# Two matmuls and a fold in place of three matmuls for 28 of layer 0's projections

## Chip, cores and metric

The kernel runs on one core of one Trainium2 chip. The metric is the device time of one execution in microseconds (us); the time before is the median of three runs.

## The reference

A two-layer decoder trunk over 256 tokens of width 2048, all in float32. Layer 0 is what the change touches:

```python
def recurrent_mixers(h, w_in, ...):
    proj = h @ w_in                                   # 2048 -> 6144 columns
    x_lru, y_lru, q_h, f_h, v_h, g_h = jnp.split(proj, list(IN_SPLITS), axis=-1)
    lru = rg_lru(causal_depthwise_conv(x_lru, conv_w, conv_b), w_a, b_a, w_i, b_i, lam)
    lru = lru * jax.nn.gelu(y_lru.astype(F32), approximate=True)
    hg = hgrn2(q_h, f_h, v_h, g_h, lower_bound, g_norm)   # 8 heads of 128 columns
    return jnp.concatenate([lru, hg], axis=-1) @ w_out
```

`h` is the RMS-normed input. `hgrn2` is a gated linear recurrence with a 128x128 state per head. A residual add and a squared-ReLU MLP follow; layer 1 has attention in the mixer's place.

## The kernel before

Every float32 product is made of float32r parts: a weight unit (one tile of 128x2048, 1 MB) is loaded to `raw`, ACT casts it to `hi` (L117) and DVE forms `lo = raw - hi` (L118), each in two halves in layer 0. The activations stand in `bufa` as `[hi | lo]`, 256 columns each. A product keeps hi*hi, hi*lo and lo*hi. `raw`, `hi` and `lo` have three buffers each, so the cast of one unit waits until PE has read the `hi` of the unit three before it, and the subtraction waits for that unit's `lo`.

A projection of layer 0 (`project`, for one block of 128 output features) takes one unit: 16 weight blocks of 128x128, each the stationary operand against 256 token columns. Two helpers do it. `direct` runs three matmuls of 256 columns per block, all into columns 0 to 255 of a PSUM bank `p`. `cross` runs one matmul of 512 columns for the block's `hi` (both halves of the activation at once, over the whole bank) for all 16 blocks, and then one of 256 columns for each block's `lo`, into the bank's second half; the two halves of the bank must be added afterwards. That fold is in `scaled`: ACT copies the second half to `t1` (L443), DVE adds the first (L444) and multiplies by the norm's factor (L445). After `direct` one DVE multiplication (L440) is all. Before, all of layer 0 uses `direct`; layer 1's q and k projections use `cross`.

The steps of layer 0 stand in the string `ORDER`: `v0 h0 x0 h1 x1 h2 x2 h3 x3 v1 h4 x4 h5 x5 h6 x6 h7 x7 g0 y0 y1 y2 y3 g1 y4 y5 y6 y7`. `h` is a head of `hgrn` (three projections: q, f, g), `x` an input block of the RG-LRU (one projection, `lru_in`), `y` its gate branch, `g` the two groups of recurrence gates, `v` the values of four heads each, computed by token (two banks at once, 96 matmuls of 512 columns). The projections, gates and value groups are chained in this order on PE (`mm`). A head's own small matmuls are not: L475, seven levels of L491, L486, L515 to L517 and the transposes L529 are put among the projections by a scheduler, which writes one fixed order for every engine. Between two levels of a head DVE updates the head's mask result (L494) and its operand `qk` (L508); the levels 32 and 64 are copied into `st` by ACT (L499, L501), the last by L487.

The banks: pool `pmm` has three, used in turn by projections, gates and value groups; pool `psc` has two named `pl` for the levels (also used by half of the gates of `g1`) and one each of `po`, `pd` and `pt`. The values of `v0` and `v1` share one buffer `vg`, so ACT's read-out of `v1`'s two banks (L361) waits until head 3's last products with the old values (L516, L517) are through.

Of the kernel before, what the change touches and what calls it, by code (L numbers as in the profile page):

```python
# [41 lines left out]
def trunk_kernel(ctx, tc, head, x, xtok, cols, tab, masks, pos, fin, w_in, w_gate, w_out, w_qkv, w_o, w1, w2, out):  # L42
# [154 lines left out]
    def unit(src, i):  # L197
        u = at[1]
        assert units[u][0] is src and units[u][1] in (None, i), (u, i)
        at[1] += 1  # L200
        if u + 2 >= at[0]:
            fetch()
        return made.pop(u)
# [54 lines left out]
            mm(p, h, mov[:, S:], start=False, stop=False)  # L258
            mm(p, l, mov[:, :S], start=False, stop=last)

    HA, XA, YA = direct, direct, direct

    def split_to(dst, src, gain=None):
        if gain is None:
            h, l = dst[..., :S], dst[..., S:]
            A.copy(h, src)
            V.tensor_tensor(l, src, h.bitcast(F32), OP.subtract)  # L267
        else:
            A.activation(dst[:, :S], src, AF.Copy, scale=gain)  # L269
            V.scalar_tensor_tensor(dst[:, S:], src, gain, dst[:, :S].bitcast(F32),  # L270
                                   op0=OP.mult, op1=OP.subtract)
# [92 lines left out]
    def project(src, i, mov, acc=None):  # L364
        w = unit(src, i)
        p = pmm.tile([P, 512], F32, name="p")
        jobs = [(k, mov[:, k], k == 0, k == KB - 1) for k in range(KB)]
        (acc or cross)(p, w, jobs)
        return p
# [67 lines left out]
    def scaled(p, z, acc=None):  # L437
        with urgent():
            if acc is direct:
                V.tensor_tensor(z, p[:, :S], rs, OP.mult)  # L440
            else:
                t = wk.tile([P, S], F32, name="t1", bufs=2)
                A.copy(t, p[:, S:])  # L443
                V.tensor_tensor(z, p[:, :S], t, OP.add)  # L444
                V.tensor_tensor(z, z, rs, OP.mult)  # L445
# [10 lines left out]

    def hgrn(hd, vg):
        u0 = 18 + (hd // 4) * 16 + (hd % 4) * 3
        oml = omlb[:, hd:hd + 1]
        qk = wk.tile([P, 2 * S], F32, name="qk", bufs=3)  # L460
        qp, kq = qk[:, :S], qk[:, S:]
# [76 lines left out]
    xc = wk.tile([P, 8, S], F32, name="xc", bufs=1)  # L538

    def lru_in(b):  # L540
        p = project(w_in, b, bufa, XA)
        xp = wk.tile([P, S + 4], F32, name="xp", bufs=1)
        V.memset(xp[:, :4], 0.0)
        scaled(p, xp[:, 4:], XA)
        A.activation(xc[:, b], xp[:, 4:], AF.Identity, bias=col("conv_b", b), scale=col("conv_w", 24 + b))
        for i in range(3):
            V.scalar_tensor_tensor(xc[:, b], xp[:, 1 + i:1 + i + S], col("conv_w", 8 * i + b), xc[:, b],
                                   op0=OP.mult, op1=OP.add)
        split_to(bufb[:, b], xc[:, b])
# [39 lines left out]
    for step in ORDER.split():  # L589
        i = int(step[1])  # L590
        if step[0] == "v":
            vgroups[i] = tokens_group(w_in, 30, rt) if i else vfirst
        elif step[0] == "h":
            hgrn(i, vgroups[i // 4])
        else:
            {"x": lru_in, "y": lru_out, "g": lru_gates}[step[0]](i)
# [557 lines left out]
```

## Time and profile before

| | |
|---|---|
| median of 3 runs | 2142.7 us (2142.47 to 2142.79) |
| profiled execution | 2142.28 us, span 2140.5 us |
| busy PE / PE weight loads / DVE / ACT | 2129.8 / 1826.2 / 1823.9 / 1280.6 us |
| granted TensorE clock | 0.999 |
| HBM read | 485.95 MB, 228 GB/s over the span |

PE starts layer 0's projections at 28.3 us and ends them at about 331 us. How to read the rows: "busy" of PE counts pipelined matmuls whose ends are modelled, so what a matmul costs is read from the distance between starts. An arrow `<-` behind an idle time names what ended it. In the timeline, equal instructions that follow each other are one row with `xN`.

### The profile page before, as it was taken

How to read it: one execution, taken by the hardware profiler on the slowest of the kernel's cores; microseconds unless marked ns; L12 is line 12 of the kernel's file. 1: busy time of each engine (PE TensorE's matmuls, PEld its weight loads, DVE VectorE, ACT ScalarE, POOL GpSimd, SP SyncE). 2: the span in 40 equal slices, each digit the busy share in tenths (PEclk: the TensorE clock that was granted, in tenths of full speed). 3: DMA queues.
4: the chain of work that ended last, by engine and by line, in shares of the span. 5: the costliest groups of instructions: out<-in, count | busy, mean ns of one | idle time of the engine just before them, and what ended most of it. 6: DMA issues, size and time to landing. Idle time of an engine off the chain costs nothing.

```text
span 2140.5 us, 27726 instructions
## 1 busy us (share of the span) xinstructions
PE 2129.8 (99%) x10994; PEld 1826.2 (85%) x10994; DVE 1823.9 (85%) x2137; ACT 1280.6 (60%) x1405; POOL 65.3 (3%) x81
## 2 busy tenths in 40 slices
PE   9999999999999999999999999999999999999998
PEld 8999998888888888888888888888888888888887
DVE  7776789988888888888988897898988988888897
ACT  7444485666566566557665545466755755755764
POOL 0000000000000000000000000000000000000000
PEclk9999999999999999999999999999999999999999
DMA  8544446788878878887785456467878788788885
GB/s 325 175 159 158 147 157 229 217 249 261 251 233 265 256 246 245 273 248 231 245 263 199 171 161 233 158 209 245 250 234 282 238 248 260 255 244 243 272 263 157
DMA packets 68738, 489.85 MB, mean 229 GB/s; under 512 B 7664, under 2 KB 7920, under 8 KB 10112
## 3 DMA queue, kind: packets, MB, share of 16 engines
q1 hardware_dynamic: 57600, 410.89, 52.0%
q0 software_dynamic: 10720, 76.58, 19.6%
q8 instruction: 86, 1.41, 0.3%
q10 hardware_dynamic: 288, 0.61, 0.1%
q14 instruction: 44, 0.36, 0.0%
HBM read 485.95 MB, written 2.10 MB: 228 GB/s over the span
## 4 chain that ended last, share of the span: by engine, by line
PE 97%; DVE 1%; ACT 1%; DMA 0%; issue 0%; SPq 0%
PE p L208 65%; PE po L208 14%; PE pd L208 13%; PE pl L211 2%; PE pl L491 1%; PE pt L208 1%; DVE lo L118 0%; ACT hi L117 0%; DMA both_in<-in_head 0%; PE pl L922 0%; PE po L943 0%; PE pd L935 0%; PE pd L475 0%; PE pl L921 0%; ACT bufa L269 0%; PE po L944 0%
## 5 line engine op out<-in xcount | busy, mean ns | idle before, releaser
L117 ACT CAST hi<-raw 128x2048 fp32r<-128x2048 f32 (+1 forms) x444 | 673.8, 1539 | 556.0 <-PE p L208 329.0
L118 DVE TENSOR_TENSOR lo<-raw,hi 128x2048 fp32r<-128x2048 f32 (+1 forms) x444 | 805.8, 1828 | 172.3 <-ACT hi L117 156.1
L208 PE MATMUL p<-hi,bufb 128*128 128x512 f32 x1264 | 405.1, 391 | 0.0
L208 PE MATMUL p<-bufa,hi 128*128 128x256 f32 (+1 forms) x1792 | 367.3, 318 | 0.1
L208 PE MATMUL p<-hi,bufa 128*128 128x512 f32 x1136 | 363.6, 390 | 0.7 <-ACT bufa L269 0.7
L208 PEld LDWEIGHTS p<-bufa,hi 128*128 128x128 f32 x1792 | 295.0, 191 | 18.6 <-DVE hz L440 0.3
L208 PEld LDWEIGHTS p<-hi,bufb 128*128 128x128 f32 x1264 | 237.4, 188 | 49.2 <-DVE bufb L267 0.3
L208 PE MATMUL p<-bufa,lo 128*128 128x256 f32 x1152 | 256.4, 287 | 0.0
L118 DVE TENSOR_TENSOR lo<-s,hi 128x2048 fp32r<-128x2048 f32 x108 | 246.9, 2286 | 9.1 <-ACT hi L117 6.8
L208 PEld LDWEIGHTS p<-hi,bufa 128*128 128x128 f32 x1136 | 213.1, 188 | 44.9 <-ACT bufa L269 0.9
L208 PE MATMUL p<-lo,bufb 128*128 128x512 f32 x632 | 246.4, 390 | 0.0
L117 ACT CAST hi<-s 128x2048 fp32r<-128x2048 f32 x108 | 206.6, 1913 | 48.0 <-PE po L208 23.0
L208 PE MATMUL p<-lo,bufa 128*128 128x512 f32 x568 | 221.7, 390 | 0.1
L208 PEld LDWEIGHTS p<-bufa,lo 128*128 128x128 f32 x1152 | 189.9, 191 | 2.7
L208 PEld LDWEIGHTS p<-lo,bufb 128*128 128x128 f32 x632 | 118.8, 188 | 24.2
L208 PEld LDWEIGHTS p<-lo,bufa 128*128 128x128 f32 x568 | 106.7, 188 | 22.5 <-DVE lo L118 0.5
L208 PE MATMUL po<-hi,bufb 128*128 128x512 f32 (+1 forms) x320 | 102.4, 387 | 0.0
L208 PE MATMUL pd<-hi,bufa 128*128 128x512 f32 x288 | 95.3, 393 | 0.0
L208 PE MATMUL p<-hi,formx 128*128 128x512 f32 x288 | 94.9, 390 | 0.0
L208 PE MATMUL p<-hi,formh 128*128 128x512 f32 x288 | 94.6, 389 | 0.0
L118 DVE TENSOR_TENSOR lo<-t,hi 128x2048 fp32r<-128x2048 f32 x36 | 82.4, 2288 | 13.0 <-ACT hi L117 13.0
L208 PE MATMUL po<-hi,bufa 128*128 128x512 f32 x256 | 85.0, 393 | 0.0
(319 smaller groups left out, 3010.5 us busy)
## 6 DMA issues: line engine op xcount, KB each, us to landing
raw<-in_w SPq DMA_DIRECT2D x224, 1024.0 KB, 6.6
raw<-in_w_qkv SPq DMA_DIRECT2D x46, 1024.0 KB, 4.9
raw<-in_w_in SPq DMA_DIRECT2D x45, 1024.0 KB, 4.9
t<-in_w SPq DMA_DIRECT2D x32, 1024.0 KB, 6.4
t<-in_w POOLq DMA_DIRECT2D x32, 1024.0 KB, 9.0
s<-in_w POOLq DMA_DIRECT2D x32, 1024.0 KB, 9.2
raw<-in_w_out SPq DMA_DIRECT2D x15, 1024.0 KB, 5.0
raw<-in_w_o SPq DMA_DIRECT2D x15, 1024.0 KB, 4.8
```

The costliest lines, as they stand in the source:

```text
L117: casts[:] = [after(A.copy(h, w), [])]
L118: i = V.tensor_tensor(l, w, h.bitcast(F32), OP.subtract)
L208: chain[:] = [after(T.matmul(*args, **kw), chain)]
L211: chain[:] = [after(T.transpose(out_, in_, ident), chain)]
L491: T.matmul(pl[:, j], kq[:, js], halves(qp[:, js], c, True), start=True, stop=True)
```

## The change

Seven of eight heads (their q, f and g projections) and seven of eight recurrence inputs go from `direct` to `cross`, with the fold: 28 projections. Head 7, input 7, the eight `y` projections and the gates keep `direct`.

```diff
-    HA, XA, YA = direct, direct, direct
+    PAIRWISE = 7
+    of_head = lambda i: cross if i < PAIRWISE else direct
+    YA = direct
...
     def hgrn(hd, vg):
         u0 = 18 + (hd // 4) * 16 + (hd % 4) * 3
+        HA = of_head(hd)
...
     def lru_in(b):
+        XA = of_head(b)
         p = project(w_in, b, bufa, XA)
```

The scheduler writes another order for layer 0 (from the first MLP on, every engine's order is as before). Three places of it follow. In the changed kernel line numbers are 2 to 4 higher: the copy of the fold is L445, its addition L446, the level L494 and L511, the read-out of the values L363.

ACT, from the casts after `v1` to the read-out of `v1`'s two banks, before (`p_1755` and `p_1756` are those banks; `hz_1946` and `hz_2007` come from the first two projections after `v1`, `st_1541` belongs to head 3):

```order
L117 CAST hi_1952<-raw_1950 128x1024 x2
L499 COPY st_1541<-pl_1579 32x2x32 x2
L239 ACTIVATE qk_1888<-hz_1946 128x256
L501 COPY st_1541<-pl_1587 64x2x64
L487 COPY st_1541<-pl_1594 128x128
L117 CAST hi_2101<-raw_2099 128x1024 x2
L239 ACTIVATE f_2009<-hz_2007 128x256
L239 ACTIVATE qk_1888<-hz_2007 128x256
L361 ACTIVATE vg_1885<-p_1755,nr2_318 128x512
L361 ACTIVATE vg_1885<-p_1756,nr2_318 128x512
```

and now (`p_1547` and `p_1548` are `v1`'s banks; `p_1873` and `p_1925` are the third and fourth projection after `v1`, those of head 4's g and of x4; `st_1359` belongs to head 3):

```order
L445 COPY t1_1907<-p_1873 128x256
L239 ACTIVATE g_1911<-hz_1906 128x256
L117 CAST hi_1973<-raw_1971 128x1024 x2
L502 COPY st_1359<-pl_1397 32x2x32 x2
L445 COPY t1_1960<-p_1925 128x256
L504 COPY st_1359<-pl_1405 64x2x64
L490 COPY st_1359<-pl_1412 128x128
L549 ACTIVATE xc_386<-xp_1958,c__88 128x256
L268 CAST bufb_81<-xc_386 128x256
L117 CAST hi_2021<-raw_2019 128x1024 x2
L363 ACTIVATE vg_1677<-p_1547,nr2_318 128x512
L363 ACTIVATE vg_1677<-p_1548,nr2_318 128x512
```

Before, two projections (`p_1897`, `p_1958`) have been read when the value banks are; now four have, `p_1689` and `p_1737` (head 4's q and f) ahead of these rows and the two shown.

DVE, at the end of the first two projections after `v1`, before (`p_1897`, `p_1958`; `lo_1953` and `lo_2102` are weights of later units, `qk_1413` is head 3's):

```order
L118 TENSOR_TENSOR lo_1892<-raw_1889,hi_1891 128x1024 x2
L267 TENSOR_TENSOR bufb_81<-g_1341,bufb_81 128x256
L494 COPY_PREDICATED st_1541<-msk_181,pl_1572 128x8x16
L508 TENSOR_TENSOR qk_1413<-qk_1413,tot16_1570 128x2x8x16
L440 TENSOR_TENSOR hz_1946<-p_1897,nr_333 128x256
L508 TENSOR_TENSOR qk_1413<-qk_1413,tot8_1577 128x2x4x32
L118 TENSOR_TENSOR lo_1953<-raw_1950,hi_1952 128x1024 x2
L465 SCALAR_TENSOR_TENSOR qk_1888<-hz_1946,omlb_373,qk_1888 128x256
L508 TENSOR_TENSOR qk_1413<-qk_1413,tot4_1585 128x2x2x64
L440 TENSOR_TENSOR hz_2007<-p_1958,nr_333 128x256
L118 TENSOR_TENSOR lo_2102<-raw_2099,hi_2101 128x1024 x2
```

and now (`p_1689`, `p_1737`; `lo_1732` and `lo_1868` are the weights of the units three behind these two, `qk_967` is head 2's and `qk_1257` head 3's):

```order
L118 TENSOR_TENSOR lo_1732<-raw_1729,hi_1731 128x1024 x2
L511 TENSOR_TENSOR qk_967<-qk_967,tot4_1113 128x2x2x64
L446 TENSOR_TENSOR hz_1722<-p_1689,t1_1723 128x256
L447 TENSOR_TENSOR hz_1722<-hz_1722,nr_333 128x256
L497 COPY_PREDICATED st_1359<-msk_181,pl_1362 128x128
L511 TENSOR_TENSOR qk_1257<-qk_1257,f_1352 128x2x128
L468 SCALAR_TENSOR_TENSOR qk_1680<-hz_1722,omlb_373,qk_1680 128x256
L497 COPY_PREDICATED st_1359<-msk_181,pl_1369 128x64x2
L511 TENSOR_TENSOR qk_1257<-qk_1257,tot128_1367 128x2x64x2
L525 TENSOR_SCALAR hs_1130<-hs_1130 128x2
L118 TENSOR_TENSOR lo_1868<-raw_1865,hi_1867 128x1024 x2
L328 TENSOR_SCALAR rs2_1135<-hs_1130 128x2
```

Before, the reading of a projection's bank (L440) stands ahead of the next two-half subtraction (L118); now it (L446) stands behind it. The row of `p_1737` follows after one L497; that of `p_1873` stands behind two halves of L118, an L269 and an L497, that of `p_1925` behind two halves and an L511.

PE, where head 7 ends, before (`qk_2914` is head 7's operand, `p_3504` is the third of the four `y` projections ahead of `g1`):

```order
L208 MATMUL p_3504<-bufa_80,lo_3365 128x256
L208 MATMUL p_3504<-bufa_80,hi_3364 128x256 x2
L486 MATMUL pl_3095<-qk_2914 128x128
L208 MATMUL p_3504<-bufa_80,lo_3365 128x256
L208 MATMUL p_3504<-bufa_80,hi_3364 128x256 x2
```

and now (`qk_2550` is head 7's operand, `p_3207` the last `y` projection ahead of `g1`, `pl_3276` the first gate of `g1`, `pt_2442` a transpose of head 6):

```order
L494 MATMUL pl_2709<-qk_2550 128x64 x2
L208 MATMUL p_3207<-bufa_80,hi_3067 128x256
L208 MATMUL p_3207<-bufa_80,lo_3068 128x256
L208 MATMUL p_3207<-bufa_80,hi_3067 128x256 x2
L208 MATMUL p_3207<-bufa_80,lo_3068 128x256
L494 MATMUL pl_2716<-qk_2550 128x64 x2
L494 MATMUL pl_2724<-qk_2550 128x64 x2
L532 MATMUL pt_2442<-tab__180,ho_2422 128x128 x2
L489 MATMUL pl_2731<-qk_2550 128x128
L518 MATMUL po_2734<-vg_1677,st_2678 128x128
L208 MATMUL pl_3276<-bufb_81,hi_3134 128x256 x2
```

Before, the last steps of head 7 stand inside projections; now its levels 32 and 64, L489 and L518 stand one behind the other at the gates' start.

## The prediction, blind

> **What bounds the kernel now.** I read the page first: the busy times and the chain that ended last.
>
> ```profile
> PE 2129.8 (99%) x10994; PEld 1826.2 (85%) x10994; DVE 1823.9 (85%) x2137; ACT 1280.6 (60%) x1405; POOL 65.3 (3%) x81
> PE 97%; DVE 1%; ACT 1%; DMA 0%; issue 0%; SPq 0%
> ```
>
> PE is the chain. A busy PE could still be one that is held up inside its pipeline, so the waits of PE come next, and then the stretch that changes.
>
> ```profile
> PE po L280 <- DVE e L409: 1.1, 1, 1.1
> PE p L208 <- ACT bufa L269: 0.7, 1, 0.7
> PE pl L208 <- ACT gr L239: 0.5, 1, 0.5
> ...
> core 0: us, PE busy (x) PEld busy (x) DVE busy (x) ACT busy (x) POOL busy (x), PEclk, DMA share, GB/s
> 100.00:200.00 100.00, 99.88 (x754) 95.61 (x753) 70.57 (x164) 43.77 (x82) 0.00 (x0) 1.00 0.46 157
> 200.00:300.00 100.00, 100.00 (x846) 99.89 (x845) 79.38 (x197) 56.97 (x116) 0.00 (x0) 1.00 0.45 150
> ```
>
> PE waits 2.3 us in the whole span, the clock is full, DMA is half used, DVE has 20 to 30 us free in 100 and ACT about 50. So time saved on PE in layer 0 is saved at the end, and time that PE loses there is lost at the end. The question is what the edit saves on PE and what new waits it makes.
>
> **The matmuls.** A `direct` block now, and a `cross` projection as layer 1 runs it:
>
> ```profile
> 100.90 0.28 PE L208 MATMUL p<-bufa,lo 128*128 128x256 f32 x1
> 101.02 0.40 PE L208 MATMUL p<-bufa,hi 128*128 128x256 f32 x2
> 101.26 0.28 PE L208 MATMUL p<-bufa,lo 128*128 128x256 f32 x1
> ...
> 1204.97 3.82 PE L208 MATMUL p<-bufa,hi 128*128 128x512 f32 x16
> 1208.62 2.08 PE L208 MATMUL p<-bufa,lo 128*128 128x256 f32 x16
> 1210.54 0.39 PE L208 MATMUL p<-bufa,hi 128*128 128x512 f32 x1
> ```
>
> From start to start a direct block takes 101.26 - 100.90 = 0.36 us, a projection 16 x 0.36 = 5.76 us. The cross projection takes 1210.54 - 1204.97 = 5.57 us: 3.65 for the 16 wide ones, 1.92 for the others. That is 0.19 us less; 28 projections: **-5.3 us**. The wide matmul costs nearly twice the narrow one, so the third less instructions bring 3%, not a third.
> [...]
>
> **The fold's own work.** Per projection one ACT copy more, and one DVE addition more; 0.37 and 0.42 us by layer 1's rows (below). That is 28 x 0.37 = 10.4 us of ACT and 28 x 0.42 = 11.8 us of DVE in 200 us that have some 100 and 50 us free: off the path where another bank is free. With no cover it would be on the path, which is the next part. The weights are no new wait: `lo` is first needed 3.65 us into the projection instead of at once, and the `hi` buffer is free after the wide pass already, 1.9 us ahead of the end, as layer 1's next cast shows:
>
> ```profile
> 1208.82 2.00 ACT L117 CAST hi<-raw 128x1024 fp32r<-128x1024 f32 x2 [3.23 <-PE p L208]
> ```
>
> **The banks after `v1`.** The order shows that `v1`'s two banks are read after the copies of four projections. With three banks in `pmm`, the projections of head 4 (q, f, g), x4 and head 5's q have one bank among them: each must wait until the fold of the one before has read it, four times. Before, this is so twice. What one such change of hands costs with `direct`, and with a fold where the bank is not short:
>
> ```profile
> 164.81 0.28 PE L208 MATMUL p<-bufa,lo 128*128 128x256 f32 x1
> 164.93 0.56 PE L491 MATMUL pl<-qk 128*128 128x64 f32 x4
> 165.13 0.42 DVE L440 TENSOR_TENSOR hz<-p,nr 128x256 f32<-128x256 f32 x1 [2.10 <-PE p L208]
> 165.61 0.51 PE L208 MATMUL p<-bufa,hi 128*128 128x256 f32 x2
> ...
> 1210.79 0.37 ACT L443 COPY t<-p 128x256 f32<-128x256 f32 x1
> 1210.79 2.36 DVE L118 TENSOR_TENSOR lo<-raw,hi 128x1024 fp32r<-128x1024 f32 x2 [0.51 <-PE p L208]
> 1213.07 0.42 DVE L444 TENSOR_TENSOR hz<-p,t 128x256 f32<-128x256 f32 x1
> ```
>
> With `direct`, DVE sits idle for PE's last matmul, reads the bank at once, and PE goes on at 165.61 instead of 164.93: 0.68 us, of which the L491s fill 0.37: 0.3 lost. I count 0.6 for the two.
> In layer 1 the same last matmul that lets the fold start also releases the `lo` buffer. The two halves of L118 start at that moment, and the addition comes behind them: it ends at 1213.49, 2.95 us after the next projection began in its free bank (1210.54). With 0.06 for the hand-over (165.55 to 165.61), a projection in the *same* bank waits 3.0 us. The order has the same sequence at all four places: L118 twice, then the addition. More stands between, and PE has small matmuls there that it must do anyway:
>
> ```profile
> 111.03 0.39 PE L486 MATMUL pl<-qk 128*128 128x128 f32 x2
> 111.25 0.39 PE L515 MATMUL po<-vg,st 128*128 128x128 f32 x2
> 111.47 0.56 PE L491 MATMUL pl<-qk 128*128 128x64 f32 x4
> 111.84 0.36 PE L208 MATMUL p<-bufa,hi 128*128 128x256 f32 x1
> ...
> L494 DVE COPY_PREDICATED st<-msk,pl 128x128 f32<-128x128 int8 x40 | 14.2, 356 | 17.8 <-PE pl L491 17.6
> L508 DVE TENSOR_TENSOR qk<-qk,tot 128x256 f32<-128x256 f32 x48 | 20.5, 427 | 2.0 <-PE pl L491 2.0
> L267 DVE TENSOR_TENSOR bufb<-g,bufb 128x256 fp32r<-128x256 f32 x8 | 3.4, 420 | 0.0
> 301.19 0.16 DVE L326 TENSOR_SCALAR rs<-hs 128x2 int32<-128x2 int32 x1
> ```
>
> L486 and L515 take 0.22 each, a level's L491s 0.37. First and fourth place: 3.0 + 0.43 (a level's L508 ahead of the addition) = 3.4, but L486 and another head's L491s follow that L508 on PE and end at 3.6; they and L515 and the level before fill 1.18; 2.4 lost each. Second: 3.0 + 0.36 + 0.16 - 0.37 = 3.15. Third: 3.0 + 0.42 + 0.36 - 0.37 = 3.4. Sum 11.35, less the 0.6 of before: **+10.7 us**. If the addition came first on DVE a place would cost some 0.28 + 0.37 + 0.42 + 0.2 = 1.3 us instead, and less than the fill at two of them: about +2 in all. Upwards, waits that also hold the casts: +14.
>
> **The end of head 7.** Head chains run later now (the fold lengthens each head), and head 7's last levels stand bare in front of `g1`, which needs the `pl` banks behind them. I take the start of level 16 as 0. With its 0.37 and the five matmuls' 0.6, `p_3207` ends at about 1.2, and only then may ACT cast the unit three on.
>
> ```profile
> L117 ACT CAST hi<-raw 128x1024 fp32r<-128x1024 f32 x112 | 111.7, 1046 | 70.2 <-issue 40.5 <-PE p L208 26.9 <-DMA raw<-in_w_in 1.0
> L526 ACT ACTIVATE ho<-po,hr 128x128 f32<-128x128 f32 x16 | 4.9, 356 | 0.4 <-DVE hr L331 0.4
> L239 ACT ACTIVATE q<-q 128x256 f32<-128x256 f32 x8 | 3.4, 419 | 2.9 <-DVE q L582 2.9
> L499 ACT COPY st<-pl 32x64 f32<-32x64 f32 x16 | 3.2, 200 | 10.4 <-PE pl L491 10.3
> L501 ACT COPY st<-pl 64x128 f32<-64x128 f32 x8 | 2.1, 259 | 1.3 <-PE pl L491 1.1
> ```
>
> ACT's order there is two cast halves, L526 twice, one L239, L499 twice, L501, and L515 on PE needs that L501: 1.25 + 2.0 + 0.7 + 0.4 + 0.4 + 0.26 = 5.0. PE reaches the gate at 5.3 instead of at its own work's 2.34 (0.37 + 0.6 + 2 x 0.37 + 3 x 0.22): **+3.0 us**; if ACT is ahead, only the chain of two L508s counts, +1; if it is behind, +5.
>
> **Sum.** -5.3 + 10.7 + 3.0 = +8.4. The profiled execution took 2142.28 us (span 2140.5 and 1.78 around it), the median is 0.4 above it: 2142.7 + 8.4 = **2151.1 us**. From the first MLP on the order is unchanged, PE never waits there, and the delay is passed on whole.
>
> **Rivals.**
> - *The folds are quick or hidden.* If DVE takes the additions ahead of L118, the terms are -5.3 + 2 + 1 to 3: 2140.4 to 2142.4, no change. For it: DVE has time. Against it: DVE runs its written order, and 1210.79 to 1213.49 shows that sequence at work. Chance 0.13.
> - *Only the matmuls count*, so the kernel is faster: 2142.7 - 5.3 = 2137.4. The value banks would have to be read early enough to leave three banks, and head 7's end would have to be covered. For it: layer 1's cross projections follow each other without a gap. Against it: the order of ACT and PE. Chance 0.07. [...]
> - *The clock drops.* The pauses come four times in some 27 us. At the start, before PE has been busy, its matmuls are slower:
>
> ```profile
> L280 PE MATMUL po<-nr 128*128 128x128 f32 x18 | 4.0, 417 | 1.1 <-DVE e L409 1.1
> L529 PE MATMUL pt<-tab__180,ho 128*128 128x128 f32 x16 | 4.0, 273 | 0.0
> ```
>
> Twice 3.5 us at half speed would add some 4 us, at each pause 7: 2155 to 2158. Chance 0.08; the pauses are partly filled. [...]
>
> **How the numbers follow.** The forecast's mechanism has the remaining 0.72. Its own ends are -5.3 + 7 + 1 = 2145.4 and -5.3 + 14 + 5 = 2156.4. The range, 2144.5 to 2157.5, adds part of the clock case above and a little of the case of hidden folds below; it leaves out the rest of that and the faster one. A measurement here tells from no change about 0.2%, 4.3 us: faster is below 2138.4, slower above 2147.0. Slower: most of the forecast's 0.72 (some 0.05 of it falls between 2145 and 2147) and the clock's 0.08, 0.76; the same: 0.05 + 0.12, 0.17; faster: 0.07.
>
> **What would show it.** In the profile after: projections at 5.57 us from start to start where nothing stands between; four pauses of PE of 3 to 4 us after `v1` (between about 158 and 190 us), each ended by the DVE row of the fold's addition, with two L118 halves directly ahead of it; about 3 us lost ahead of `g1`, ended by ACT's `st`; PE busy as before from the MLP on. Wrong: additions that start within 1 us of the last matmul; pauses elsewhere in layer 0 (the head chains' other levels), which I count at nothing since projection matmuls stand between them; a granted clock under 1.

## The result and the profile after

The changed kernel takes 2158.07 us (median of 5 runs, 2157.03 to 2159.71), the kernel before on the same chip 2142.63 us (2142.15 to 2142.79): ratio 1.0072, 95% interval 1.0061 to 1.0082. That is slower by 15.4 us, where 8.4 us were forecast, and 0.6 us above the range. The profiled execution took 2159.71 us and is the slowest of the five: what is read from the profile explains the 17.4 us between it and before's profiled 2142.3 us, of which the medians have 15.4.

The page of the kernel after, busy times and chain:

```profile
PE 2135.5 (99%) x10546; PEld 1810.0 (84%) x10546; DVE 1832.0 (85%) x2165; ACT 1290.1 (60%) x1433; POOL 65.3 (3%) x81
PE 96%; DVE 2%; ACT 1%; DMA 1%; issue 0%; DVEq 0%; ACTq 0%
```

448 matmuls fewer, and PE is busy for 5.7 us longer (2129.8 before): either PE waits inside its pipeline or its matmuls are slower. The waits of PE (total us, times, longest):

```profile
PE p L208 <- DVE hz L446: 5.6, 2, 3.0
PE pl L489 <- DVE qk L511: 3.2, 2, 1.6
PE pl L494 <- DVE hr L333: 1.4, 1, 1.4
PE po L518 <- ACT st L504: 0.7, 2, 0.3
PE pl L489 <- ACT st L504: 0.6, 1, 0.6
PE pl L494 <- DVE qk L511: 0.5, 1, 0.5
```

All rows of that view add up to 14.0 us, against 2.3 before: 11.7 more. L446, L489 and L518 are the four places after `v1`, 9.5 us in all; the two rows of L494 and the L489 that waits for ACT are head 7's end, 2.5 us. The second place as the timeline shows it:

```profile
171.20 0.56 PE L494 MATMUL pl<-qk 128*128 128x64 f32 x4
171.40 0.37 ACT L445 COPY t<-p 128x256 f32<-128x256 f32 x1 [0.24 <-PE p L208]
171.40 2.36 DVE L118 TENSOR_TENSOR lo<-raw,hi 128x1024 fp32r<-128x1024 f32 x2
...
173.94 0.42 DVE L446 TENSOR_TENSOR hz<-p,t 128x256 f32<-128x256 f32 x1
174.42 0.80 PE L208 MATMUL p<-bufa,hi 128*128 128x512 f32 x1 [2.66 <-DVE hz L446]
```

This is the sequence of the forecast, row for row: ACT's copy is there at once, both halves of L118 start with the release of `lo`, and the addition ends 2.96 us after them. From PE's own end (171.20 + 0.37) to 174.42 it is 2.85 us; 3.15 were forecast. The fourth place looks different:

```profile
195.04 0.56 PE L494 MATMUL pl<-qk 128*128 128x64 f32 x4
195.94 0.49 PE L518 MATMUL po<-vg,st 128*128 128x128 f32 x2 [0.35 <-ACT st L504]
198.05 0.49 PE L489 MATMUL pl<-qk 128*128 128x128 f32 x2 [1.61 <-DVE qk L511]
```

With 0.37 for the four L494 and 0.22 for the two L518, PE is late by 0.53 and then 1.89 us, 2.42 in all. The first place (L494 at 159.36, L518 at 160.26, L489 at 162.37) comes to the same 2.42, the third (L494 at 183.97, the projection at 187.51) to 3.17. The view of waits has less, 9.5 for the four: its idle time begins at the modelled end of the last matmul (195.60 for the four L494 from 195.04), which lies 0.2 us behind the moment at which the next could have started (195.41, since four L494 take 0.37 from start to start where nothing waits).

What the waits do not hold is in the granted clock. The windows of the next block begin and end at the steps of the clock that this trace shows, or whole multiples of its shortest stretch at half clock, 3.413 us, from one; columns are length, PE busy (and its instructions), clock, DMA share and GB/s:

```profile
159.90:163.31 3.41, 1.45 (x10) 1.00 0.64 192
163.31:166.73 3.42, 3.42 (x9) 0.50 0.64 268
170.14:173.55 3.41, 1.61 (x15) 1.00 0.00 0
173.55:180.38 6.83, 5.96 (x14) 0.50 0.46 154
183.79:187.21 3.42, 0.73 (x7) 1.00 0.00 0
187.21:190.62 3.41, 3.11 (x7) 0.50 0.73 250
194.03:197.45 3.42, 2.05 (x16) 1.00 0.00 0
197.45:200.86 3.41, 2.81 (x15) 1.00 0.66 173
313.50:316.91 3.41, 2.24 (x15) 1.00 0.48 204
316.91:320.32 3.41, 3.41 (x18) 0.50 0.60 163
```

Behind three of the four places, and behind head 7's end, the granted clock is 0.50: 17.1 us, of which PE is busy for 3.42 + 5.96 + 3.11 + 3.41 = 15.9. What that costs is an estimate, half of the busy time: 8.0 us are lost. The 16 wide matmuls behind the third place bear it out: from 187.51 to 192.69 they take 5.18 us, against 3.65 at full clock, 1.53 more for their 3.11 us at half clock. The fourth place brings no fall: 1.00 behind it.

### The profile page after: what moved, and what is told of

The parts are those of the page before. It is cut to its first block, busy times and chain, and to the rows that moved or that the text cites. A ratio compares the mean times of both kernels' runs of the same rounds, so it can differ in the third digit from the quotient of the medians.

```text
span 2157.8 us, 26889 instructions
## 1 busy us (share of the span) xinstructions
PE 2135.5 (99%) x10546; PEld 1810.0 (84%) x10546; DVE 1832.0 (85%) x2165; ACT 1290.1 (60%) x1433; POOL 65.3 (3%) x81
## 4 chain that ended last, share of the span: by engine, by line
PE 96%; DVE 2%; ACT 1%; DMA 1%; issue 0%; DVEq 0%; ACTq 0%
PE p L208 64%; PE po L208 13%; PE pd L208 13%; PE pl L211 2%; DVE lo L118 1%; PE pt L208 1%; PE pl L494 1%; ACT hi L117 1%; DMA raw<-in_w 0%; PE pl L926 0%; PE po L947 0%; PE pd L939 0%; DMA both_in<-in_head 0%; PE pd L478 0%; PE pl L925 0%
## 5 line engine op out<-in xcount | busy, mean ns | idle before, releaser
L118 DVE TENSOR_TENSOR lo<-raw,hi 128x2048 fp32r<-128x2048 f32 (+1 forms) x444 | 805.0, 1827 | 194.2 <-ACT hi L117 168.3
L208 PE MATMUL p<-bufa,hi 128*128 128x512 f32 (+1 forms) x1344 | 314.1, 369 | 5.6 <-DVE hz L446 5.6
L208 PEld LDWEIGHTS p<-bufa,hi 128*128 128x128 f32 x1344 | 240.1, 192 | 41.0 <-DVE hz L446 5.9
L118 DVE TENSOR_TENSOR lo<-s,hi 128x2048 fp32r<-128x2048 f32 x108 | 246.8, 2285 | 9.8 <-ACT hi L117 7.6
L208 PE MATMUL p<-bufa,lo 128*128 128x256 f32 x1152 | 192.6, 288 | 0.0
L208 PEld LDWEIGHTS p<-bufa,lo 128*128 128x128 f32 x1152 | 162.9, 191 | 4.9
L118 DVE TENSOR_TENSOR lo<-t,hi 128x2048 fp32r<-128x2048 f32 x36 | 82.4, 2288 | 12.8 <-ACT hi L117 12.8
```

Of the source, the lines that this page charges most:

```text
L118: i = V.tensor_tensor(l, w, h.bitcast(F32), OP.subtract)
L208: chain[:] = [after(T.matmul(*args, **kw), chain)]
```

## Experiments

Times are medians; each is compared with the kernel before on the same chip (2142.4 to 2142.8 us). Diffs are against the changed kernel unless the text names another. The scheduler writes each kernel an order of its own, so a difference is that of the edit and of its order together. A theory A in the expectations takes the waits that an order shows, mostly with the clock behind them, for the whole of the loss; the rivals see the lag of the head chains or the folds as the cause. "Bare" levels are those of a head with no projection matmuls between them, "cover" is such matmuls.

**The lag paid elsewhere.** Two buffers for the values, so that `v1`'s banks are read early and the places after `v1` have a second bank:

```diff
-    vgs = ... tile_pool(name="vgs", bufs=1)
+    vgs = ... tile_pool(name="vgs", bufs=2)
```

> The changed kernel with two buffers for the values, so that the read-out of v1's two banks waits for no head and the four projections after v1 have three banks again. Theory A (the bank shortage is the cause): the four pauses of PE after v1, 10.6 us in the changed kernel's trace, and the three low-clock stretches behind them go, the end of head 7 stays: 2142.6 - 5.3 + 3.4 + 1.7 = 2142.4 us. Rival B (the head chains are too slow with the fold, and the pauses only were where that lag was paid): the lag is paid at the end of head 7 instead, where the written order now has five levels of it bare in a row; at 1.3 to 1.5 us each with the copies behind them 10 us or more, and the clock falls there: about 2150 us.

2151.26 us, ratio 1.004 (1.0025 to 1.0055), as the rival had it. The pauses after `v1` are gone, and the time is lost ahead of `g1`, where head 7's levels now stand bare:

```profile
296.62 0.68 PE L494 MATMUL pl<-qk 128*128 128x64 f32 x4 [1.94 <-DVE qk L511]
...
300.24 1.09 PE L494 MATMUL pl<-qk 128*128 128x64 f32 x4 [2.94 <-DVE qk L511]
...
302.14 1.08 PE L494 MATMUL pl<-qk 128*128 128x64 f32 x4 [0.81 <-DVE qk L511]
```

Four L494 take 1.08 us from 300 on, where they take 0.56 at full clock: the clock is at half for 17.07 us there. Without the one-bank places 6.7 of the 15.4 us come back; 8.7 stay, and the waits ahead of `g1` grow from 2.5 to 8.7 us (7.5 for L511 and 1.2 for L504). So those places are a part of the loss, and the head chains are late at their end without them. One more execution of the same kernel, for that stretch:

> Placeholder for the two-buffer kernel as it ran before: one look at whether its half-clock stretch ahead of g1 comes again in every execution. Theory A: 13.6 to 17.1 us at half clock ahead of g1, 2149.8 to 2152.9. Rival (the stretch was chance): no stretch in this execution, some 2147.

2151.4 us, with a granted clock of 0.995 over the span as in the first execution, and 7.4 us of waits for L511, where that had 7.5.

**Pauses filled.** Eight small matmuls of no use into bank `pd` behind each of the projections q, f, g of head 4 and x4:

```diff
+    def fill(here, n=8):
+        if here:
+            f = psc.tile([P, P], F32, name="pd", bufs=1)
+            for _ in range(n):
+                mm(f, ident, ident, start=True, stop=True)
```

> The changed kernel with eight 128x128 float32 matmuls of the identity with itself behind each of the four projections that share one bank, into the bank pd, which nobody reads: some 1.8 us of PE work in each pause. Theory A (the pauses pull the granted clock down, and that is the 7 to 8 us which the sum of the waits doesn't have): the pauses still end with the fold's addition, the clock stays at 1 until the end of head 7, and 6.2 us go: about 2152 us. Rival (the clock falls for another reason, the wide matmuls for one): the low stretches stay and the extra work costs at least nothing: 2158 us or more.

2155.4 us, ratio 1.006 (1.0045 to 1.0075). The clock stays at 1.0 after `v1` (150 to 200 us), but the scheduler writes another order, PE waits for 8.7 us in all, 4.5 of them now ahead of `g1`, and the clock is at half for 6.83 us there. That the clock holds where the pauses are filled fits idle time as the cause of its fall; the time lies between the two expectations, so as a price of the clock it is inconclusive.

**Fewer heads.** Heads and inputs 0 to 3 alone, and 4 to 6 alone:

```diff
-    PAIRWISE = 7
+    PAIRWISE = 4
```

```diff
-    of_head = lambda i: cross if i < PAIRWISE else direct
+    of_head = lambda i: cross if 4 <= i < PAIRWISE else direct
```

> Heads and inputs 0 to 3 alone take two matmuls and the fold (16 projections). The written order still reads v1's banks late, so that four projections share one bank, but these use three narrow matmuls and one DVE multiplication. Theory A (what costs is the fold behind two halves of the subtraction in a single bank): 16 x 0.19 = 3.0 us saved, four changes of hands at 0.3 for two, no low clock, no bare levels at head 7's end: 2142.6 - 3.0 + 0.6 = 2140.2 us. Rival (late heads cost by themselves): some 2.5 us at each of four places and the clock: 2150 us.

> Heads and inputs 4 to 6 alone take two matmuls and the fold (12 projections). The order gives one change of hands in a single bank behind a fold, and the bare levels of head 7 ahead of g1 as in the changed kernel. Theory A: -2.3 for the matmuls, +2.3 for the one place (2.9 less 0.6), +3.4 for head 7 and up to 1.7 for each low-clock stretch: 2146 to 2149 us. Rival (a cost per fold): 12/28 of the 15.4 us, 2149.2, without pauses of that size at these places.

The first takes 2140.02 us, ratio 0.9988 (0.9979 to 0.9997): 2.5 us faster than before, and the version that beats both. Its waits of PE add up to 3.0 us and its clock never falls in layer 0 (columns as in the windows above):

```profile
30.00:330.00 300.00, 298.78 (x2194) 1.00 0.49 168
```

So 16 x 0.19 = 3.0 less 0.7 of waits is what is measured: the matmul term is right. The second takes 2150.94 us, ratio 1.0038 (1.0024 to 1.0053), above theory A's range: 7.5 us of waits, and 6.83 us at half clock. That is also above the rival of a cost per fold (2149.2), which the first four heads refute: 16 folds and no loss. Alone, the first four gain 2.5 and the other three lose 8.4 us, 5.9 together; both at once lose 15.4. So the three heads after `v1` lose time by themselves, and 9.5 us more appear only when the heads ahead of `v1` are changed too.

**The addition ahead of L118.** One more rule for DVE: the subtractions of a unit come behind the fold written before them.

```diff
             i = V.tensor_tensor(l, w, h.bitcast(F32), OP.subtract)
+            after(i, folds)
...
-                V.tensor_tensor(z, p[:, :S], t, OP.add)
+                folds[:] = [after(V.tensor_tensor(z, p[:, :S], t, OP.add), [])]
```

> The changed kernel, with one more rule for DVE's order: the two halves of a weight subtraction (L118) come behind the addition of the fold that was written before them. Theory A (the lag of the head chains is what costs; the banks after v1 only show a part of it): the one-bank places lose some 1 us each instead of 2.7, DVE's order then leaves six levels of head 7 bare ahead of g1, at 1.3 to 1.9 us each, and the clock falls there: 2142.6 - 5.3 + 4 + 9 + 3 = 2153, 2149 to 2156. Rival B (the two halves ahead of the addition are the cause, as the prediction's case of quick folds has it): 2140.4 to 2142.4, clock 1.0.

2160.68 us, ratio 1.0083 (1.0066 to 1.01): slower than the change itself. But at the first transposes in layer 0's output projection (L211 before, at 358.26 us) it is 13.8 us late (372.06), the change 16.8 (375.07) and the two-buffer kernel 10.4 (368.67); the other 5.3 us of its profile's 19.1 come later. Lines are two higher here. The first place, and the kernel's largest waits:

```profile
159.13 0.42 DVE L448 TENSOR_TENSOR hz<-p,t 128x256 f32<-128x256 f32 x1
159.36 0.63 PE L496 MATMUL pl<-qk 128*128 128x64 f32 x4 [0.81 <-DVE qk L513]
159.46 1.22 DVE L119 TENSOR_TENSOR lo<-raw,hi 128x1024 fp32r<-128x1024 f32 x1
159.79 0.48 PE L210 MATMUL p<-bufa,hi 128*128 128x512 f32 x1
```

```profile
PE pl L496 <- DVE qk L513: 9.1, 8, 3.0
PE p L210 <- DVE lo L119: 2.4, 1, 2.4
```

The addition now ends before the next projection wants the bank, no place after `v1` waits for more than 0.81 us, and the clock holds there. But head 7's levels stand bare ahead of `g1` as with two value buffers, with 13.65 us at half clock, and the rule costs a wait for `lo` of 2.4 us and a half-clock window in layer 1. The prediction's rival of quick folds (2140.4 to 2142.4) falls: in layer 0 quick folds bring back 3 us of the 16.8. Theory A's 2149 to 2156 is missed too, by the part behind layer 0, which I had not seen coming.

**The two halves of the change apart.** The fold's work with the matmuls of before (the maximum of the result and its copy is the result):

```diff
-                A.copy(t, p[:, S:])
-                V.tensor_tensor(z, p[:, :S], t, OP.add)
+                A.copy(t, p[:, :S] if acc is folded else p[:, S:])
+                V.tensor_tensor(z, p[:, :S], t, OP.max if acc is folded else OP.add)
```

and the new matmuls without the fold:

```diff
+                if part == "h":
+                    mm(p, h, mov, start=first, stop=False, skip_group_check=True)
+                else:
+                    mm(p[:, :S], l, mov[:, :S], start=False, stop=last, skip_group_check=True)
...
-            if acc is direct:
+            if acc in (direct, wide):
```

> The 28 projections run their three 256-column matmuls per block again, but the fold's work stays: ACT copies the bank's result and DVE takes the larger of the result and its copy, which is the result. So PE has the work of before, ACT and DVE the work of the change, and each head's chain the fold's latency. Theory C (the lag comes from PE: projections that are 0.19 us shorter, and that the scheduler spaces the head steps by, leave the later heads too little cover): 2142 to 2145, clock 1.0. Rival D (the lag comes from the folds: each head's chain is longer by the copy, the addition and the subtraction halves ahead of it): 2150 to 2160, with pauses of 10 us or more in layer 0 and a half-clock stretch.

> The other half alone: the 28 projections run the 512- and the 256-column matmuls, with the second one added into the bank's first half, and the read-out is the one multiplication of before. Left out is the product of hi weights with lo activations, which the wide matmul still computes into the second half. So PE has the work of the change, ACT and DVE that of before. Theory C: 2142.6 - 5.3 + 12.5 of bare levels ahead of g1 (as with two value buffers) + 2 to 6 for the clock = 2152 to 2156, range 2149 to 2158. Rival D: 2137.3 to 2140, clock 1.0.

2151.6 us (ratio 1.0042, 1.0029 to 1.0056) and 2149.29 us (1.0032, 1.002 to 1.0044). Each half alone is slower, by 9.0 and 6.7 us, 15.7 together and 15.4 in the change. The first is in rival D's range, without its pauses of 10 us (4.7 us more than before), and the second in theory C's, so neither C nor D alone is enough. The waits stand at other places than in the change, so that the two losses add up to it may be chance. The largest waits of layer 0 in the first, which saves PE nothing:

```profile
PE pl L497 <- DVE qk L514: 2.1, 3, 0.8
PE po L521 <- ACT st L507: 1.5, 2, 1.1
```

And the end of head 7 in the second, which leaves DVE and ACT the work of before, with its clock (columns as above):

```profile
298.30 0.63 PE L503 MATMUL pl<-qk 128*128 128x64 f32 x4 [1.27 <-DVE qk L520]
300.12 0.63 PE L503 MATMUL pl<-qk 128*128 128x64 f32 x4 [1.20 <-DVE qk L520]
302.26 1.08 PE L503 MATMUL pl<-qk 128*128 128x64 f32 x4 [1.51 <-DVE qk L520]
```

```profile
297.40:300.82 3.42, 1.26 (x8) 1.00 0.68 237
300.82:311.06 10.24, 7.35 (x31) 0.50 0.34 127
```

The levels are bare though no fold exists: with shorter projections the order leaves head 7 without cover. In both, a pause is followed by half clock: two stretches of 3.41 us in the first, 10.24 us in the second.

**Fillers at the end.** Two value buffers, and fillers behind head 7's levels:

```diff
+            if hd == 7:
+                fl = psc.tile([P, P], F32, name="pd", bufs=1)
+                fills = [after(last, [])]
+                for _ in range({1: 8, 2: 10}.get(c, 3)):
+                    fills = [after(T.matmul(fl, ident, ident, start=True, stop=True), fills)]
```

> The kernel with two value buffers, with matmuls of no use behind the levels of head 7 (eight behind the first, ten behind the second, three behind each later one; 0.21 us each), so that PE is idle for less time there while DVE and ACT do the same work. Theory A on the clock (the idle time brings it down, and it costs 2.1 us at the gates of g1 that run at half speed and some 2 us in the levels): no half-clock stretch, 2151.3 - 4.2 = 2147, range 2146 to 2149. Rival (the clock costs nothing where DVE sets the pace, or the fillers delay the chain by what the clock gives): 2150 to 2153.

2150.47 us (2147.36 to 2151.29), ratio 1.0032 (1.002 to 1.0044). The median is in the rival's range. A wait of 1.63 us is left unfilled and the clock still falls, for 6.83 us, all of them filled with matmuls. It is inconclusive on the price of the clock; PE waits for 6 us less (4.3 in all) and the time moves by 0.8, as it would where DVE's chain sets the pace.

**More cover.** Two value buffers, and `g1` behind y6:

```diff
-    ... y3 g1 y4 y5 y6 y7
+    ... y3 y4 y5 y6 g1 y7
```

> The kernel with two value buffers, and g1 three y projections later in ORDER (y0 to y6 ahead of g1, y7 behind it), so that head 7's levels have 17 us more of PE work to stand in. Theory C: the whole gain of the matmuls is left, 2142.6 - 5.3 + 1 to 3 = 2138 to 2140. Rival (g1 is then the last thing before the output projection, and its gates, scans and the products of blocks 4 to 7 are late for it): 2142 to 2150, with PE waiting for DVE behind y7.

2144.73 us, ratio 1.0009 (1.0 to 1.0018): not theory C's 2138 to 2140 but the rival's range, though PE waits for nothing behind y7. In this order y4 to y6 multiply inputs that have not been through `g1`'s gates and scan, so that part of the computation is changed. 6.5 us come back against the two-buffer kernel; its granted clock is 0.998 over the span, that of the two-buffer kernel 0.995 and that of the kernel before 0.999. With that reserve, cover ahead of `g1` is what the end of head 7 lacks.

**Pauses and the clock.** The kernel before, with pauses of many lengths in layer 1:

```diff
+            mm(p[:, :P], ident, ident, start=True, stop=True, skip_group_check=True)
+            A.copy(idle[:, 0], p[:, :32])
+            for i in range(n):
+                nc.gpsimd.tensor_copy(idle[:, (i + 1) % 2], idle[:, i % 2])
+            mm(p[:, :32], ident, idle[:, n % 2], start=True, stop=True, skip_group_check=True)
```

> The kernel before, with a pause of PE put in front of the q projection of 15 of layer 1's 16 heads, some 12 us or more apart: a small matmul, an ACT copy of its result, one to seven GpSimd copies one after the other, and a small matmul that needs the last of them. So the idle times grow from about 1 to some 4 us, with nothing else changed. Theory A (about 2 us of idle time within one 3.41 us window are enough for the clock to fall): pauses below 1.7 us leave the clock at 1.0, between 2 and 3.4 us some bring it down, according to how they lie on the windows, and each fall lasts 3.41 or 6.83 us and costs half of what of it is busy. Rival (only a gap as long as a whole window, 3.4 us, brings it down): no half-clock stretch behind any pause under 3.4 us.

2220.2 us. Of 15 pauses, 12 are followed by half clock. Four of them by window (a pause, and what came behind it):

```profile
1143.53:1146.95 3.42, 2.20 (x13) 1.00 0.36 153
1146.95:1150.36 3.41, 3.41 (x22) 1.00 0.92 308
1191.32:1194.73 3.41, 1.47 (x13) 1.00 0.27 113
1194.73:1198.15 3.42, 2.44 (x7) 0.50 0.62 180
1198.15:1201.56 3.41, 3.41 (x10) 0.50 0.30 127
1211.80:1215.21 3.41, 1.39 (x9) 1.00 0.13 55
1215.21:1218.63 3.42, 3.30 (x9) 0.50 0.90 307
1218.63:1222.04 3.41, 3.41 (x21) 1.00 0.02 5
1385.88:1389.29 3.41, 2.19 (x11) 1.00 0.47 115
1389.29:1392.70 3.41, 3.41 (x23) 1.00 0.47 197
```

In every one of the 12, PE was busy for 1.47 us or less of the 3.41 us ahead of the fall; in the three others for 2.19 or more. The rival falls: the pause that ends at 1160.06 is 2.37 us long, and the clock is at half from 1160.60 on. How long it stayed there differed. In this run it was back at 1.00 after one window in which PE was busy for 3.30 us (the second fall above), and at half for a second one behind windows with 0.77, 2.44 (the first fall above) and twice 3.17; in the change one window with 3.11 was all, and behind the fillers of head 7's end the clock was at half for 6.83 us though PE was busy throughout.

PE's busy time alone does not tell the two cases apart. The kernel of g and x below has both:

```profile
176.21:179.62 3.41, 1.69 (x13) 1.00 0.40 171
179.62:186.45 6.83, 6.59 (x19) 0.50 0.47 154
305.92:309.33 3.41, 1.68 (x14) 1.00 0.47 197
309.33:312.75 3.42, 3.42 (x31) 1.00 0.62 180
```

So read in the change, in this run, and ahead of the falls with two value buffers (1.47), with the addition first (0.66), in the fold without wide matmuls (1.86 and 0.93), in the wide ones without fold (1.26) and in the kernel of g and x, the clock was at half behind all 19 windows at full clock with 0.01 to 1.61 us of PE work, and behind three of the nine with 1.68 to 2.52 (1.69, 1.86 and 2.24). These are counts of the windows named, not a limit that any run shows.

**Which projections.** q and f of heads 0 to 6 alone, and g of heads 0 to 6 with the inputs 0 to 6 alone (`GA` is used for g):

```diff
-        HA = of_head(hd)
+        HA, GA = of_head(hd), direct        # XA = direct in lru_in
```

```diff
-        HA = of_head(hd)
+        HA, GA = direct, of_head(hd)
```

> Only the q and f projections of heads 0 to 6 change, 14 of the 28; g and the recurrence inputs keep the three matmuls of 256 columns. The written order has two one-bank places with a fold after v1 (f waits for q's fold, g for f's) and head 7's levels covered. Theory A (the loss is made at such places, 2.7 us each, and by the clock behind them): 2142.7 - 2.7 + 5.4 = 2145.4, with 1.7 us more for each half-clock window of 3.41 us: range 2144 to 2149, nothing lost ahead of g1. Rival (the q and f folds lengthen the chain of each head, and the loss goes by the chain wherever it shows): lag of 8 us or more, part of it ahead of g1, 2149 to 2154.

> The other 14: only the g projections of heads 0 to 6 and the recurrence inputs 0 to 6 change, which no head chain waits for. The written order has one one-bank place with a fold after v1 (x4 waits for the fold of head 4's g) and head 7's levels covered. Theory A: 2142.7 - 2.7 + 2.7 = 2142.7, and 1.7 to 3.4 us more if the clock falls behind it: 2142 to 2146. Rival (the loss goes by the number of folds, whichever they are): half of the change's 15.4 us, 2150.

2149.82 us (ratio 1.0032, 1.0021 to 1.0043) and 2145.65 us (1.0016, 1.0007 to 1.0025). The first has its two places, 5.0 us by L446, each with a half-clock window behind it; the median is just above theory A's range and at the rival's lower end, and 1.7 us are lost at `g1`, where theory A had nothing. The second is in theory A's range, with that same 1.7 us and with another place than I named: the last level of a head (L489), 1.6 us. Equal numbers of folds cost 7.4 and 3.2 us, so the loss does not go by their number.

**The y projections too.** The first four heads and inputs, with all y projections, and with y0 to y5:

```diff
-    YA = direct
+    YA = cross
```

```diff
+        YA = cross if b < 6 else direct
```

> The kernel of the first four heads and inputs, with the eight y projections as 512- and 256-column matmuls too: 24 projections, none of them in the stretch after v1 or of heads 4 to 7. Theory A: 2142.6 - 24 x 0.19 = 2138.0, range 2137.4 to 2139.4, clock 1.0. Rival (the folds of y0 to y3 take ACT and DVE from head 7's last levels, or the shorter y projections leave head 7 bare ahead of g1): pauses ahead of g1, 2140 to 2145.

> The first four heads and inputs and the y projections 0 to 5, 22 projections; y6 and y7, the last two ahead of the output projection, are read by one DVE multiplication again. Theory A: 2142.7 - 22 x 0.19 = 2138.5, range 2137.7 to 2139.8, clock 1.0, and less than 1 us of waits at the start of the output projection. Rival (the DVE work of y5's fold is still in the way of the subtractions and of y7's read-out there): a pause of 2 to 5 us at the output projection's start and a half-clock stretch, 2141 to 2147.

2146.63 us (ratio 1.0019, 1.001 to 1.0028) and 2147.24 us (1.002, 1.0011 to 1.0028); theory A is wrong for both. The rivals have the size nearly right (each median is just above its range); that of the first had named another place, ahead of `g1`. The output projection waits for the read-out of a bank, here in the first and in the second kernel:

```profile
PE p L208 <- DVE z L446: 5.3, 1, 5.3
```

```profile
PE p L208 <- DVE z L441: 4.8, 1, 4.8
```

In the second no fold is left in that bank: the read-out is late in DVE's order, behind subtractions and the scans of `g1`. Why six shorter y projections bring it there is open.

**The three terms over the kernels.** The two kernels with fillers and the one with another computation are left out. Gain of the matmuls (0.19 us each), waits of PE above the 2.3 of before, and half of PE's busy time at half clock in layers 0 and 1 (the estimate of above), from one profiled execution each; beside it that execution's distance to before's 2142.3 us and that of the medians.

| kernel | matmuls | waits | clock | sum | profiled | medians |
|---|---|---|---|---|---|---|
| after | -5.3 | 11.7 | 8.0 | 14.4 | 17.4 | 15.4 |
| two value buffers | -5.3 | 8.1 | 5.6 | 8.4 | 10.6 | 8.7 |
| first four | -3.0 | 0.7 | 0 | -2.3 | -2.6 | -2.5 |
| heads 4 to 6 | -2.3 | 5.2 | 3.1 | 6.0 | 6.4 | 8.4 |
| addition first | -5.3 | 13.9 | 6.3 | 14.9 | 19.1 | 18.1 |
| fold without wide | 0 | 4.7 | 3.4 | 8.1 | 10.7 | 9.0 |
| wide without fold | -5.3 | 6.5 | 3.7 | 4.9 | 8.3 | 6.7 |
| q and f | -2.7 | 6.3 | 3.4 | 7.0 | 8.9 | 7.4 |
| g and x | -2.7 | 3.4 | 3.3 | 4.0 | 5.2 | 3.2 |
| four and all y | -4.6 | 6.5 | 2.0 | 3.9 | 4.3 | 3.9 |
| four and six y | -4.2 | 6.1 | 1.5 | 3.4 | 3.6 | 4.8 |

Only the first four heads keep the clock, and only they are faster than before. The sum stays up to 4.2 us below the profile, most where PE waits often. A part of that rest is the 0.2 us ahead of each idle time that the view of waits does not hold, and 0.1 us more for the first matmuls behind it (two L489 take 0.32 instead of 0.22 up to the next start, at 198.05): as an estimate from these rows, 0.2 to 0.3 us for each wait, 1.8 to 2.7 for the 9 more waits of the change. No run isolates it.

## Why the prediction was wrong

1. **The matmuls, -5.3: right.** 16 of them gave 2.5 us with 0.7 us of waits.
2. **The fold's work is covered ahead of `v1`: right.** No wait of PE there, and the first four heads keep their gain.
3. **The banks after `v1`, +10.7: place and size right, the sequence at two of four.** Counted as the forecast counts, from where PE's own work would have ended, the four places cost 2.42, 2.85, 3.17 and 2.42, 10.9 us; 2.4, 3.15, 3.4 and 2.4 were forecast, 11.35. Less the 0.6 of before that is +10.3. The middle two are ended by L446 behind two L118. At the other two the last wait is for the level's L511, not for the addition: the fill that I counted ended late as well.
4. **The end of head 7, +3.0: size nearly right, releaser wrong.** From level 16 (310.68) PE reaches the gate (316.77) after 6.1 us instead of 5.3: +3.7. (Its own work adds up to 2.37 us, not the 2.34 of the forecast, which changes nothing.) The wait was to end with ACT's `st` behind two casts; of the 2.5 us of idle time 1.9 end with DVE. For 1.4 of them the trace names a step of a head's normalisation (L333), whose result that L494 does not read; its `qk` comes from the L511 before, which ended at 313.14, 0.15 us ahead of it.
5. **The clock: the step that failed.** The sum had no term for it. "The clock drops" stood as a rival with a chance of 0.08, at 4 us for two falls and 7 for one at each pause; its 2155 to 2158 is where the time came out. The term is estimated at 8.0 us from the profile, and the forecast without it, 2151.1, is 7.0 short of the median. With the other terms as measured, -5.3 + 10.3 + 3.7 + 8.0 = 16.7; the first transposes in layer 0's output projection (L211) start at 358.26 us before and at 375.07 now, 16.8 later. So the waits of the forecast stand, and the clock is what it lacks. No run shows the rival's stretch of 3.5 us; the change's profile has 3.41, 6.83, 3.41 and 3.41 us at 0.50 in its place. The reason I gave, "the pauses are partly filled", took the pauses one by one and was my estimate of what the clock bears. What the runs show: each of the 19 windows of 3.41 us that were read with 1.61 us of PE work or less was followed by half clock. A pause of 2.4 to 3.4 us, as forecast, leaves 1.0 us of work or less where it falls into one such window; the fourth place left 2.05 in its window and brought no fall.
6. **Terms that do not simply add.** I took the one-bank places and head 7's end as two separate losses. Take the first away (two value buffers, or the addition first) and the waits at the second grow from 2.5 to 8.7 us in either kernel (7.5 ended by `qk`, 1.2 by `st`). That the chain through the heads has one end, for which PE waits earlier or later, fits this and is argued from it. Either half of the change is enough to uncover it.
7. **The delay passed on whole: nearly.** 16.8 us of delay in layer 0's output projection are 17.3 in the whole span; some 0.5 us come in layer 1, where the forecast had none. The range reached 2157.5 only by ends of the other terms (+14, +5) that did not occur and by part of the clock's case, so that the time lies no more than 0.6 above it is luck. By the forecast's own cases its chances add up to 0.75 for slower and 0.18 for the same, not 0.76 and 0.17.

Of the falls the traces show lengths and starts. They last 3.41 us or a multiple of it, up to 17.07 with two value buffers, and the change's four begin whole multiples of 3.413 us apart, 45 of them from 163.31 to 316.91. Work in the 3.41 us ahead did not always keep the clock: 1.47 us of it did not with two value buffers and in the pause kernel.

What stays open: how much of the 8.0 us would come back with the clock held and the order unchanged, since fillers changed the order each time; and why the lag of the head chains moves between the places after `v1` and the end.

## What to carry to other kernels

Where PE is the bound with its clock full, price each new pause twice: by its length, and by the half clock that may follow it; in the change 17.1 us at half clock, an estimated 8.0 us lost, came beside 12.0 us of waits at the five places. The matmuls' 0.19 us of 5.76 per projection helped here only where another engine's chain was not about to become the one waited for: change the stretch that has slack (here the first four heads) and leave the one that paces a chain. Moving a wait away by a buffer or an order shows how much of it was the cause and how much only the place: here 6.7 of 15.4 us came back. Count a wait from the start that PE's own work would have allowed, not by idle time alone.

## What was not expected of the hardware

The clock fell after every window of 3.41 us with 0.01 to 1.47 us of PE work in the pause kernel, 12 of them, and after 1.45, 1.61 and 0.73 us in the change; it held at 2.00 and 2.05 in the change and at 2.19, 2.20 and 2.52 in the pause kernel. One window with 2.24 us of busy time, with small matmuls ahead of `g1` (313.50 in the windows of the result), was followed by half clock all the same, and of the two windows with 1.69 and 1.68 us in the kernel of g and x only the first was. What tells these apart was not shown; PE's busy time by modelled ends does not.
